# Two-layer hybrid encoder trunk on one core: the second half of the gated embedding moved behind the last expert, every expert's rows stored by the same transfer, and a reordered opening

## The chip, the cores and the metric

One core of a Trainium2 chip runs the whole program. The metric is device time in microseconds (us) of one execution. TensorE is written PE (PEld is its weight load), VectorE DVE, ScalarE ACT, GpSimd POOL and SyncE SP. SP issues most loads; POOL issues the indirect transfers and those that add into memory.

## The reference, cut to what is computed

512 tokens of width 1024 pass a layer norm and then two layers of this form:

```python
u = h @ w_in[i]                       # 1024 x 2560, three head groups
mix = concat([hyena, attention, pool]) @ w_out[i]
h = layer_norm(DN_ALPHA * h + mix, ln1_g[i], ln1_b[i])
y_moe = hier_moe(h, ...)              # 16 experts, every token goes to 2 of them
y_ple = sigmoid(h @ ple_wg[i] + ple_bg[i]) * (p[i] @ ple_wp[i])   # the gated embedding
h = layer_norm(DN_ALPHA * h + y_moe + y_ple, ln2_g[i], ln2_b[i])
```

An expert computes `silu(t @ w1) * (t @ w3) @ w2` with `w1`, `w3` of 1024x256 and `w2` of 256x1024, weighted by the token's gate.

## The kernel before, in words

Tokens are four tiles of 128 rows (`t` = 0 to 3). Matrix products keep nearly full float32 accuracy: `split` (L222) cuts a tensor into a rounded part `hi` (a cast on ACT) and a rest `lo` (a subtraction on DVE), and `mm3` (L215) issues three matmuls, hi x hi, hi x lo and lo x hi.

**Units.** All large weights are consumed through one list, made by `plan` (L1451). A unit is a weight slice of up to 512 KB, its loads and the matmuls that use it. `pump` (L233) issues the loads of the next units on SP and the splits of the next few; how far ahead is set by `ahead_raw` and `ahead_split`. In the expert stage this is 15 and 3 units (`P_MOE`), from expert 10 on 7 and 3 (`P_END`), from the last expert on 8 and 4 (`P_LAST`), where `cap` also stops the loads three units behind the end of the layer. `fill(n)` works off n units. Loaded slices, split parts, activations and norm gains share 34 slots of SBUF (`s4`). The compiler of the tile framework orders each engine's instructions; `behind()` and `issue_after` put instructions behind another one on the same engine's queue, without a wait between engines.

**Expert stage.** `layer` (L1518) gathers 128 rows of `h` per expert by an indirect transfer (`gather`, L1249), transposes them (`expert_x`), works four units of `w1` and `w3` (`add_expert_in`) and two of `w2` (`add_expert_out`). For experts 0 to 13 the result tile `ye` is added into the tensor `yd` in HBM by an indirect adding transfer on POOL (`scatter`, L1255). `yd` starts as a copy of the normed stream (`norm1`). The last two experts (`NL = 2`) stay on the core as two parts `yl`; `last_places` (L1414) makes one-hot matrices `hotT`, and `tail_sum` (L1420) brings their rows to the tokens with eight matmuls for each token tile (L1431), plus for the tiles in `ZPE` a float32 matmul with the identity (L1434).

**Gated embedding.** Each 512-column half of the gate has four units of 512 KB and 96 matmuls of 128x512. The first half (`add_ple(i, 0)`) comes ahead of the experts and is added into `yd` by two transfers of 512 KB on POOL (L1228). The second half is cut in two: two units after expert 3, kept in `plz`, and two after expert 12, then added into `yd` in the same way.

**End of a layer.** `load_stream` (L1407) reads `yd` back into `h` on POOL, after all that was added has landed. `finish` (L1441) then takes the tiles in turn: `tail_sum`, norm statistics (`moments`), the norm (`ln_tile`). In layer 0 these tiles feed the transposes and the projection of head 0 of layer 1 (`add_head` with `before`, L756), which works all four of its weight units for one tile before the next; in layer 1 they are stored to `out`.

**Opening.** `build` (L1640) issues on SP, in this order: tile 0 of `x` in two halves, gain and bias of the first norm as rows repeated over 128 partitions (`gain`, 512 KB each), the constants `cst` (409 KB, the identity for the transposes among them), the first head unit (384 KB), tiles 1 to 3 of `x`, and then the other units as they are pumped. Head 0 takes `start_norm` (L1492) for its norm; the statistics of tiles 1 to 3 are made on ACT directly behind tile 0. DVE clears five buffers at the start.

## Time and profile before

| | us |
|---|---|
| median of the runs | 1043.53 |
| lowest and highest of 3 runs | 1042.79 and 1048.24 |
| the profiled execution | 1045.37 |
| its span, first to last instruction | 1043.6 |

The page gives the busy time of each engine: PE 968.6 us, DVE 779.1, ACT 613.6, POOL 172.9. The span can be read as an opening up to 41.8 us (norm and head 0), the rest of layer 0's mixing part up to some 340 us, its expert stage up to 522.6 us, the passage into layer 1, the same parts again, the second expert stage up to 1016.1 us and a tail of 27.6 us. A window of the trace gives each engine's busy time and instruction count, the granted TensorE clock, and the mean busy share of the 16 DMA engines with the rate that they moved. Matmul records overlap, so the distance between two starts is the cost of one.

### The profile page before, as it was taken

How to read it: one execution, taken by the hardware profiler on the slowest of the kernel's cores; microseconds unless marked ns; L12 is line 12 of the kernel's file. 1: busy time of each engine (PE TensorE's matmuls, PEld its weight loads, DVE VectorE, ACT ScalarE, POOL GpSimd, SP SyncE). 2: the span in 40 equal slices, each digit the busy share in tenths (PEclk: the TensorE clock that was granted, in tenths of full speed). 3: DMA queues.
4: the chain of work that ended last, by engine and by line, in shares of the span. 5: the costliest groups of instructions: out<-in, count | busy, mean ns of one | idle time of the engine just before them, and what ended most of it. 6: DMA issues, size and time to landing. Idle time of an engine off the chain costs nothing. (4 is left out here: it accounts for less than half of the span.)

```text
span 1043.6 us, 14416 instructions
## 1 busy us (share of the span) xinstructions
PE 968.6 (93%) x4869; PEld 800.6 (77%) x4870; DVE 779.1 (75%) x1301; ACT 613.6 (59%) x1046; POOL 172.9 (17%) x170
## 2 busy tenths in 40 slices
PE   4999999999989999999979999999998999999995
PEld 3887889898767788777758889898776778877762
DVE  7576897777676778887865578847678587888785
ACT  5425464655653768886843346654655386888673
POOL 1101000000222222422121000000012222333121
PEclk9999999999999999999989999999999999999997
DMA  8816121222974999999974412122186399999974
GB/s 262 239 37 142 51 71 52 71 81 68 316 242 102 306 302 311 307 292 301 285 261 114 109 56 67 51 70 83 61 302 243 94 329 302 315 300 312 293 207 161
DMA packets 156010, 197.49 MB, mean 189 GB/s; under 512 B 20296, under 2 KB 123786, under 8 KB 155925
## 3 DMA queue, kind: packets, MB, share of 16 engines
q1 hardware_dynamic: 135253, 155.58, 45.5%
q0 software_dynamic: 20672, 40.87, 15.1%
q8 instruction: 42, 0.69, 0.3%
q14 instruction: 43, 0.35, 0.1%
HBM read 182.85 MB, written 29.36 MB: 203 GB/s over the span
## 5 line engine op out<-in xcount | busy, mean ns | idle before, releaser
L225 DVE TENSOR_TENSOR wlo<-raw,whi 128x1024 fp32r<-128x1024 f32 (+2 forms) x278 | 324.1, 1182 | 66.0 <-ACT whi L224 61.1
L224 ACT CAST whi<-raw 128x1024 fp32r<-128x1024 f32 (+2 forms) x278 | 277.9, 1024 | 33.1 <-DMA raw<-in_moe_w_dram 13.9
L218 PE MATMUL e<-whi,xT 128*128 128x512 f32 x256 | 106.6, 416 | 2.7 <-ACT xT L224 1.8
L219 PE MATMUL e<-wlo,xT 128*128 128x512 f32 x256 | 103.7, 405 | 0.1
L220 PE MATMUL e<-whi,xT 128*128 128x512 f32 x256 | 101.8, 398 | 0.0
L218 PE MATMUL pj<-whi,hT 128*128 128x384 f32 x256 | 90.0, 352 | 2.3 <-ACT hT L224 1.8
L219 PE MATMUL pj<-wlo,hT 128*128 128x384 f32 x256 | 88.2, 345 | 0.3 <-DVE wlo L225 0.3
L220 PE MATMUL pj<-whi,hT 128*128 128x384 f32 x256 | 87.3, 342 | 0.6 <-DVE hT L225 0.5
L1257 POOL DMA_INDIRECT yd<-ye,rt_tok x28 | 53.1, 1895 | 187.2 <-ACT ye L1323 66.7
L868 ACT ACTIVATE prob<-sc,mx 128x512 f32<-128x512 f32 x64 | 43.7, 688 | 39.1 <-DVE mx L867 36.6
L308 POOL TENSOR_TENSOR ors<-rs_y,mhalf 128x4 f32<-128x4 f32 x8 | 8.5, 1057 | 335.3 <-DVE rs_y L307 335.3
L1251 POOL DMA_INDIRECT xe<-hd,rt_tok x32 | 48.8, 1525 | 91.4 <-PE tr L376 48.1
L218 PEld LDWEIGHTS e<-whi,xT 128*128 128x128 f32 x256 | 48.9, 191 | 12.9 <-ACT xT L224 2.2
L219 PEld LDWEIGHTS e<-wlo,xT 128*128 128x128 f32 x256 | 48.8, 191 | 11.4 <-DVE wlo L225 2.4
L220 PEld LDWEIGHTS e<-whi,xT 128*128 128x128 f32 x256 | 48.8, 191 | 10.0
L219 PE MATMUL e<-wlo,actT 128*128 128x512 f32 x128 | 51.6, 403 | 3.1 <-DVE wlo L225 3.1
L218 PE MATMUL mo<-whi,YT 128*128 128x512 f32 x128 | 53.2, 415 | 0.0
L218 PEld LDWEIGHTS pj<-whi,hT 128*128 128x128 f32 x256 | 48.9, 191 | 4.8 <-ACT hT L224 2.5
L219 PE MATMUL pl<-wlo,hT 128*128 128x512 f32 x128 | 51.4, 401 | 1.1 <-DVE wlo L225 1.1
L218 PE MATMUL pl<-whi,hT 128*128 128x512 f32 x128 | 50.8, 402 | 0.6 <-ACT whi L224 0.5
L218 PE MATMUL e<-whi,actT 128*128 128x512 f32 x128 | 47.8, 398 | 3.8 <-ACT whi L224 2.9
L218 PE MATMUL pj<-hT,whi 128*128 128x512 f32 x128 | 51.2, 404 | 0.0
(340 smaller groups left out, 2313.1 us busy)
## 6 DMA issues: line engine op xcount, KB each, us to landing
raw<-in_moe_w_dram SPq DMA_DIRECT2D x256, 256.0 KB
raw<-in_moe_w_dram SPq DMA_DIRECT2D x64, 512.0 KB
raw<-in_w_in_dram SPq DMA_DIRECT2D x96, 128.0 KB
raw<-in_w_in_dram SPq DMA_DIRECT2D x16, 512.0 KB
raw<-in_ple_wg_dram SPq DMA_DIRECT2D x16, 512.0 KB
raw<-in_w_out_dram SPq DMA_DIRECT2D x14, 512.0 KB
tabi<-c_tabi_dram POOLq DMA_DIRECT2D x8, 516.0 KB, 4.6
tabf<-c_tabf_dram POOLq DMA_DIRECT2D x8, 512.0 KB
```

The lines of the kernel that those rows point to most:

```text
L218: mm(ps, a[0], b[0], start=start, stop=False)
L219: mm(ps, a[0], b[1], start=False, stop=False)
L220: mm(ps, a[1], b[0], start=False, stop=stop)
L224: self.nc.scalar.copy(hi, src)
L225: self.nc.vector.tensor_sub(lo, src, hi.bitcast(F32))
L308: nc.gpsimd.tensor_tensor(out, y, self.mhalf[:, :n], op=OP.pow)
L868: nc.scalar.activation(p[:, c], o, AF.Exp, bias=mx[:, c:c + 1], accum_out=sm[:, c:c + 1])
L1251: self.nc.gpsimd.indirect_dma_start(out=x, out_offset=None, in_=self.hd[:, :], in_offset=bass.IndirectOffsetOnAxis(ap=tok, axis=0), bounds ...
L1257: self.nc.gpsimd.indirect_dma_start(out=self.yd[:, :], out_offset=bass.IndirectOffsetOnAxis(ap=row, axis=0), in_=y, in_offset=None, bounds ...
```

## The change

- **Gated embedding.** The second half is no longer cut in two. Its four units follow the last expert's; the matmuls start when all four are split, one token tile after the other (24 matmuls each). The gated product stays on the core: it overwrites `pwp[1]`, and `tail_sum` adds it to `h`. The two adding transfers of this half are gone, and the first half's `plz` and the experts' `ye` share two buffers (`out4`).
- **Experts.** All sixteen store by `scatter`. `NL`, `last_places`, `own`, `yl`, `hotT` and `ZPE` with all their matmuls are gone. `load_stream` is issued behind the last expert's store and ahead of the second half's four units. `tail_sum` makes one column half's sum on ACT and adds the gated product to the other on DVE; tile 0's is queued on ACT and DVE behind the gating of token tile 2.
- **Opening.** SP issues tile 0 of `x`, two single rows of gain and bias (4 KB each), the 128 identity columns of `cst`, all four units of head 0 (two loads each in place of three, the same rows), tiles 1 to 3 of `x`, and then the rest of `cst`. PE repeats the two rows over the partitions by four float32 matmuls with a row of ones, ACT copies them out. The statistics of tiles 1 to 3 and the split of the gate weights are queued behind casts of weights; four memsets go from DVE to POOL; two small constants are made later.

```diff
 def ple_tile(self, t, c, z, o):
+    g = z if c else o
+    nc.vector.tensor_add(g, z, self.bg[:, c * 512:(c + 1) * 512])
+    act = nc.scalar.activation(g, g, AF.Tanh, scale=0.5)
+    dve = nc.vector.scalar_tensor_tensor(o, g, 1.0, self.pwp[c][t // 2][:, t % 2], op0=OP.add, op1=OP.mult)
+    self.gated[c, t] = act.ins, dve.ins
...
 def add_ple(self, i, c):
+    def second(q):
+        def f(wp):
+            st["w"].append(wp)
+            if q < 3:
+                yield 0.01
+                return
+            for t in range(NT):
+                ps = self.ps("pl")
+                for n, x in enumerate(st["w"]):
+                    mms(ps, t, n, x)
+                self.ple_tile(t, c, ps, self.pwp[c][t // 2][:, t % 2])
+                yield 5.12
+        return f
...
 def tail_sum(self, i, t):
-    with self.behind():
-        for c in range(2):
-            for e in range(NE - NL, NE):
-                for x in range(2):
-                    nc.tensor.matmul(ps, self.hotT[e][:, t], self.yl[e][x][:, cs], ...)
-            if t in self.ZPE[i]:
-                nc.tensor.matmul(ps, self.ident, h[:, cs], start=False, stop=True)
-                nc.scalar.activation(h[:, cs], ps, AF.Copy, accum_out=sums[:, c:c + 1])
-                continue
-            nc.vector.scalar_tensor_tensor(h[:, cs], h[:, cs], 1.0, ps, ...)
+    with contextlib.ExitStack() as order:
+        if t == 0:
+            for ins in self.gated[1, 2]:
+                order.enter_context(self.tc.issue_after(ins))
+        else:
+            order.enter_context(self.behind())
+        nc.scalar.activation(self.s2([128, 512], "lnsq", BF16), h[:, :512], AF.Copy, accum_out=sums[:, 0:1])
+        nc.vector.scalar_tensor_tensor(h[:, 512:], h[:, 512:], 1.0, self.pwp[1][t // 2][:, t % 2], op0=OP.mult,
+                                       op1=OP.add, accum_out=sums[:, 1:2])
...
 def plan(self, i):
     for e in range(NE):
         self.add_expert_in(i, e)
         if e > 0:
             self.add_expert_out(i, e - 1)
-        if e in self.PLE_AT:
-            self.add_ple(i, 1, self.PLE_AT.index(e))
     self.add_expert_out(i, NE - 1)
+    self.add_ple(i, 1)
...
 def layer(self, i):
         self.fill(2)
+        self.load_stream()
+        self.fill(4)
...
 def build(self):
             if t == 0:
-                self.gb = self.gain(A["ln0_g"], A["ln0_b"])
-                nc.sync.dma_start(self.cst, self.C["cst"])
-                self.pump(0, -1)
+                for src in (A["ln0_g"], A["ln0_b"]):
+                    r = self.s4([128, 1024], "grow")
+                    nc.sync.dma_start(r[0:1], bass.AP(tensor=src.tensor, offset=src.offset, ap=[[0, 1], [1, 1024]]))
+                    rows.append(r)
+                nc.sync.dma_start(self.cst[:, :128], self.C["cst"][:, :128])
+                self.pump(3, -1)
+        nc.sync.dma_start(self.cst[:, 128:], self.C["cst"][:, 128:])
         self.setup()
+        for r in rows:
+            g = self.s4([128, 1024], "gain")
+            for c in range(2):
+                cs = slice(c * 512, (c + 1) * 512)
+                ps = self.ps("gb")
+                nc.tensor.matmul(ps, self.ones[0:1], r[0:1, cs], start=True, stop=True)
+                nc.scalar.copy(g[:, cs], ps)
```

## Rows read from the trace of the kernel before

**Rows 1.** The page's part 1: busy us, share of the span and instructions by engine.

```profile
PE 968.6 (93%) x4869; PEld 800.6 (77%) x4870; DVE 779.1 (75%) x1301; ACT 613.6 (59%) x1046; POOL 172.9 (17%) x170
```

**Rows 2.** Windows of 20 us: start:end length, busy by engine (instructions), clock, DMA share, GB/s.

```profile
0.00:20.00 20.00, 4.60 (x14) 3.18 (x15) 13.03 (x22) 8.46 (x18) 3.24 (x11) 1.00 0.86 271
...
60.00:80.00 20.00, 20.00 (x92) 16.08 (x92) 15.14 (x25) 4.15 (x6) 0.00 (x0) 1.00 0.16 46
...
380.00:400.00 20.00, 20.00 (x96) 16.42 (x95) 14.85 (x19) 11.47 (x16) 4.18 (x3) 1.00 0.86 273
...
460.00:480.00 20.00, 18.07 (x84) 13.68 (x82) 16.14 (x18) 14.46 (x20) 6.22 (x4) 1.00 0.95 297
...
520.00:540.00 20.00, 13.68 (x42) 8.40 (x42) 12.01 (x21) 8.49 (x16) 3.00 (x6) 0.83 1.02 333
```

**Rows 3.** Waits of PE up to 45 us: what ended them, us in all, times, longest.

```profile
PE tr L376 <- DMA cst<-c_cst_dram: 11.4, 1, 11.4
```

**Rows 4.** Timeline of head 0: start, us, engine, line, instruction, idle before it and its releaser.

```profile
13.91 0.69 PE L218 MATMUL pj<-whi,hT 128*128 128x384 f32 x1 [0.55 <-ACT whi L224]
...
23.11 0.84 ACT L224 CAST whi<-raw 128x768 fp32r<-128x768 f32 x1
23.39 0.52 PE L219 MATMUL pj<-wlo,hT 128*128 128x384 f32 x1
23.71 0.52 PE L220 MATMUL pj<-whi,hT 128*128 128x384 f32 x1
...
25.68 0.34 PE L218 MATMUL pj<-whi,hT 128*128 128x384 f32 x1
25.86 0.34 PE L219 MATMUL pj<-wlo,hT 128*128 128x384 f32 x1
...
42.02 0.37 ACT L797 COPY uqk<-pj 128x256 f32<-128x256 f32 x1 [1.72 <-PE pj L220]
```

**Rows 5.** Timeline of ACT in layer 0's expert stage: experts 1 and 2, a late weight.

```profile
354.62 0.38 ACT L1274 ACTIVATE act<-e 128x256 f32<-128x256 f32 x1 [0.18 <-PE e L220]
...
364.05 0.39 ACT L1274 ACTIVATE act<-e 128x256 f32<-128x256 f32 x1
...
474.60 1.05 ACT L224 CAST whi<-raw 128x1024 fp32r<-128x1024 f32 x1 [2.22 <-DMA raw<-in_moe_w_dram]
```

**Rows 6.** DMA queues in 464 to 478 us: packets, MB, share of the 16 engines' time.

```profile
q1 hardware_dynamic: 1658, 3.33, 67.8%
q0 software_dynamic: 437, 0.80, 27.0%
```

**Rows 7.** The same in 492 to 506 us, in which the adding transfers of `plz` run.

```profile
q1 hardware_dynamic: 2142, 2.83, 61.9%
q0 software_dynamic: 544, 1.05, 44.0%
```

**Rows 8.** Timeline of PE: last matmuls of expert 15 in both layers, head 0 of layer 1.

```profile
522.15 0.40 PE L220 MATMUL e<-whi,actT 128*128 128x512 f32 x1
...
541.24 0.34 PE L218 MATMUL pj<-whi,hT 128*128 128x384 f32 x1
...
1015.42 0.39 PE L219 MATMUL e<-wlo,actT 128*128 128x512 f32 x1
1015.65 0.40 PE L220 MATMUL e<-whi,actT 128*128 128x512 f32 x1
```

**Rows 9.** Groups by line: count | busy us, mean ns of one | idle before.

```profile
L1434 PE MATMUL el<-h,cst 128*128 128x512 f32 x16 | 10.2, 725 | 6.2 <-DMA h<-yd 6.2
L1207 ACT ACTIVATE plz<-plz 128x512 f32<-128x512 f32 x16 | 9.9, 632 | 36.6 <-DVE plz L1206 36.6
```

**Rows 10.** Timeline of the tail: first sum of tile 0 and last part of tile 3's norm.

```profile
1020.66 0.69 DVE L1437 SCALAR_TENSOR_TENSOR h<-h,el 128x512 f32<-128x512 f32 x1 [2.86 <-DMA h<-yd]
...
1038.27 1.41 DVE L350 SCALAR_TENSOR_TENSOR h<-ln,lnrs,gain 128x512 f32<-128x512 f32 x2 [0.82 <-POOL lnrs L308]
```

**Rows 11.** The instructions of line 1257 (an expert's store): time from issue to landing.

```profile
DMA to landing us min/median/max: 8.5/8.9/9.7
```

More of the change, by code (lines that the diff above doesn't have):

```diff
@@ L25 @@
 NE = 16
-NL = 2
 ALPHA = (2 * DEPTH) ** 0.25
@@ L205, in s2, with out4 @@
                                      padded_shape=[128, HALF * 4 // mybir.dt.size(dt)]), shape)
+    def out4(self, shape, name):
+        n = int(np.prod(shape[1:]))
+        return _view(self.slots.tile([128, n], F32, name=name, tag="out4", bufs=2), shape)
     def ps(self, name):
@@ L222, in split @@
     def split(self, hi, lo, src):
-        self.nc.scalar.copy(hi, src)
+        self.cast = self.nc.scalar.copy(hi, src).ins
         self.nc.vector.tensor_sub(lo, src, hi.bitcast(F32))
@@ L399, in setup @@
         nc.vector.memset(self.ones, 1.0)
-        self.tri_b = self.cp.tile([128, 128], BF16, name="tri_b")
-        nc.vector.tensor_copy(self.tri_b, cst[:, C_TRI:C_TRI + 128])
-        self.ones_b = self.cp.tile([128, 128], BF16, name="ones_b")
-        nc.vector.memset(self.ones_b, 1.0)
         self.qL = self.cp.tile([128, 2, 512], F32R, name="qL")
-        nc.vector.memset(flat(self.qL).bitcast(F32), 0.0)
+        nc.gpsimd.memset(flat(self.qL).bitcast(F32), 0.0)
     def setup_late(self):
@@ L421, in setup_late @@
         self.pw = self.cp.tile([128, DEPTH * 2, 128], F32, name="pw")
-        nc.vector.memset(self.pw, 0.0)
+        nc.gpsimd.memset(self.pw, 0.0)
         for half in range(2):
@@ L431, in setup_late @@
             x = self.xp.tile([128, 1024], F32, name="xe", tag="xe")
-            nc.vector.memset(x, 0.0)
+            nc.gpsimd.memset(x, 0.0)
     def lam(self):
         nc, A = self.nc, self.A
+        self.tri_b = self.cp.tile([128, 128], BF16, name="tri_b")
+        with self.behind():
+            nc.vector.tensor_copy(self.tri_b, self.cst[:, C_TRI:C_TRI + 128])
+        self.ones_b = self.cp.tile([128, 128], BF16, name="ones_b")
+        nc.vector.memset(self.ones_b, 1.0)
         lq = self.s2([128, 2, 2, 2, 64], "lq")
@@ L1018, in gate_weights @@
         gw = self.sm.tile([128, 8, 2, 20], F32R, name="gwhl", bufs=1)
-        self.split(gw[:, :, 0], gw[:, :, 1], raw)
+        with self.behind(), self.tc.issue_after(self.cast):
+            self.split(gw[:, :, 0], gw[:, :, 1], raw)
         self.gate = gw, gb
@@ L1212, in add_ple @@
+    def add_ple(self, i, c):
         nc = self.nc
         cs = slice(c * 512, (c + 1) * 512)
[L1214 to L1229 removed]
@@ L1241, in f @@
                     yield 1.28
             return f
-        for q in qs:
+        def second(q):
[11 more added lines that the diff above has]
+            return f
@@ L1245, in add_ple @@
+        for q in range(4):
             src = self.A["ple_wg"][i][q * 256:(q + 1) * 256, cs].rearrange("(k p) n -> p k n", p=128)
-            self.add([(lambda r: r, src)], [2, 512], emit(q))
+            self.add([(lambda r: r, src)], [2, 512], (first, second)[c](q))
     def gather(self, tok):
@@ L1308, in f @@
                              [x[:, c * 512:(c + 1) * 512] for x in wp], k == 0, k == 1)
[L1309 to L1321 removed]
+                if k == 1:
+                    y = self.out4([128, 1024], "ye")
                     for c in range(2):
@@ L1497, in start_norm @@
                 self.ln(self.h[0], self.h[0], self.gb, self.ln_stats(self.h[0]), True)
-                self.stats = [None] + [self.ln_stats(self.h[u]) for u in range(1, NT)]
+                with self.tc.issue_after(self.cast):
+                    self.stats = [None] + [self.ln_stats(self.h[u]) for u in range(1, NT)]
             else:
@@ L1647, in build @@
         self.h = []
+        self.cst = self.cp.tile([128, C_N], F32, name="cst")
+        rows = []
         for t in range(NT):
```

91 lines of the change are left out of this document (25 added, 66 removed).

## The prediction

> **What bounds the kernel now.** I read the page's busy times first. PE is busy 968.6 of 1043.6 us, DVE 779.1, ACT 613.6 [rows 1]. So some 75 us of PE's time are idle; the rest of the span can only shrink if PE's work shrinks, and only where PE is what a stage waits for. Next I read windows of 20 us, to see where the idle time lies [rows 2]: 15.4 us stand in the first window, 6.3 in 520 to 540 (the passage into layer 1), a like stretch at the end, and a few us in the second half of each expert stage, where the DMA share is 0.95 or more. These are the places that the change touches. Then I asked what ended the waits in each.
>
> In the opening PE waits 11.4 us for `cst` [rows 3]. The first projection starts at 13.91, the cast of the fourth head weight starts only at 23.11, and the last token tile of head 0 is copied out at 42.02 [rows 4].
>
> In the expert stage two streams run side by side: PE with 9.4 us for an expert (364.05 - 354.62 [rows 5]), and the 16 DMA engines. From about 460 us on ACT waits for weights to land, here 2.2 us at 474.6 [rows 5], with some nine more up to the end of the stage; PE has 1.9 us of idle time in that window while the DMA share is 0.95 [rows 2]. The lead of loaded weights is used up there: from then on the stage moves at the pace of the loads, not of PE. This is the point on which the prediction turns.
>
> **The opening.** Before, about 5.1 MB stand ahead of the fourth head weight on SP's queue (x 2.1, gain and bias 1.05, `cst` 0.42, head 1.57). After, it is 2.2 MB (tile 0 of x 0.52, identity 0.07, head 1.57, two rows). At the 271 GB/s of the first window [rows 2] that is 19 us against 8, so the weights come at 10 to 11 us in place of 23. What replaces the repeated loads: four float32 matmuls of one row by 512 columns. The nearest row is the identity matmul L1434: two records for each of 8 matmuls, 10.2 us in all, 1.28 us each [rows 9]. Records overlap (0.39 long at a distance of 0.23 [rows 8]), so 0.75 to 1.28 us of PE, and up to twice that at half the clock. I take 1.7, as PE is slow at the start, so 6.8 us for four, with bounds of 3 and 10. The rows come right behind tile 0's 0.5 MB, by an estimate at 4 us, so the last copy is out at 11.5 (8 to 15); then come the norm's last half, the transposes, and the first projection at about 12.4 against 13.91. The real gain is that tile 0's 24 matmuls then run without a wait.
>
> What they cost depends on the clock. Before, two starts of 128x384 lie 0.32 us apart at 23.39 and 0.18 us apart from 25.68 on [rows 4], so the engine was at 1.2 GHz first and at 2.4 after it had been busy without a long gap; the granted column reads 1.00 in both, so here the distance tells the level. Tile 0 takes 7.7 us at the one, 4.2 at the other. Then three tiles at 24 x 0.175 + 1.0 for the transposes, 5.2 us, or 5.6 with gaps, since ACT and DVE also have their norms to make. Head 0 ends at 33.5 to 37 in place of 42: a gain of 5 to 8.5, and I take 7. It lives on, as PE has no idle time from 60 to 80 us [rows 2]; if the loads behind it (forward tables, Hyena weights) can't follow, down to 4 of it are left. The Trainium skill, "TensorE: Matmul & The Clock Gate" (Part 1), says that the engine's clock is throttled by default and that activity releases it; the new matmuls would thus wake the engine ahead of tile 0, and the gain would be 8.5. The rows of this trace show the same rise, but no case with such matmuls in front.
>
> The other edits of the opening cost nothing that lasts. The four memsets wait on POOL in front of nothing but the norm's two small POOL steps and, much later, the gathers; a memset of the same size is under 1 us on DVE, and even 3 us on POOL end before tile 0's statistics do. The queue edges (`issue_after`) make no engine wait for another; the statistics of tiles 1 to 3 start at 11 us on ACT, and tile 1's norm is ready at 17, when PE is still on tile 0. On SP tiles 1 to 3 of x come behind the head weights and land at about 11 to 15 us, ahead of their use.
>
> **The expert stage: how much earlier is the last expert (call it s)?** PE loses the 96 matmuls of the two parts. Their distance is 20 us / 92 = 0.217 with few loads [rows 2], 0.23 among loads [rows 8], so 20.8 to 22 us go. If PE set the pace s would be 20.8. But the loads set it, and they lose less. The four units are 2.1 MB; at 67.8% of 14 us for 3.33 MB [rows 6], 2.85 us of all engines for 1 MB, they cost 6.0 us. The two adding transfers are 1.05 MB and took 44.0% of 14 us [rows 7], 6.2 us (at the plain price 3.0, the lower bound). Expert 14's store is added ahead of the end: 64 rows, 0.26 MB, at 4.7 to 5.9 us for 1 MB 1.2 to 1.5 us. In 380 to 400 PE was busy with the first part, the slots stayed full and the share was 0.86 [rows 2]; up to 2.8 us of load time come back there. Sum: 6.0 + 6.2 - 1.3 = 10.9, with the last item up to 13.7, and with the adding transfers at the plain price 7.5. I take s = 11.5, for both layers. PE will stand idle some 9 us more in the second half of each stage than before. The Trainium skill, "DMA: Bandwidth & Descriptors" (Anatomy of one DMA), gives a transfer 2 us and its bytes at 436 GB/s; by it the two adds occupy the engines for 2.4 us, and s would be about 7. The row of this trace says 6.2, and I go by it.
>
> **What lies behind the last expert.** Before, layer 1 ends 1043.6 - 1016.05 = 27.55 us behind expert 15's last matmul [rows 8], mostly the store's landing, the reload of `yd` and four tiles of norm. After, the second half stands first. Its weights follow the last expert's in SP's queue and land 6 us behind them; the fourth unit is needed 4 us into tile 0, so they cost 1 us at most. Token tiles 0 to 2 are 72 x 0.23 = 16.6 us; the gating of tile 2 is two DVE steps of 0.69 (as the sum in rows 10, of the same shape) around 0.63 on ACT [rows 9], with handing over 2.2. Meanwhile the last store lands (8.9 us [rows 11]) and `h` is read back, some 18 us behind the last expert: hidden by those 19, with 1 us to spare. On POOL these reads stand ahead of the norm's small steps, which need them anyway. Then four tiles of norm. Before they took 1020.66 to 1039.68, 19.0 us [rows 10]; the sums no longer wait for PE, but DVE has 0.69 for the sum and twice 1.41 for the norm in each [rows 10], 3.5, and tile 3's gating of 1.4 between; with the first tile's wait for its statistics that is 17 us at the least. I take 18. Then 3.9 us for the last store to `out`, as before. In all 0.2 + 16.6 + 2.2 + 18 + 3.9 = 40.9 us behind the last expert: 13.3 more than before. So layer 1's end moves by 13.3 - s, which is +1.8.
>
> In the passage into layer 1 the first projection came 541.24 - 522.55 = 18.7 us behind the last expert [rows 8]. After: 0.2 + 16.6 + 2.2, then 5.5 us of sum, square, POOL steps, half a norm, transposes and cast: 24.5, or 5.8 more. Between the later tiles eight matmuls of L1431 go, 1.8 us at 0.23, of which 1.3 are taken as they also hid a wait. Change 4.5 - s, which is -7.0. The clock, granted at 0.83 in 520 to 540 [rows 2] where PE was waiting, costs nothing here, as PE has work up to the norm.
>
> **Sum.** -7 (opening) - 7 (passage) + 1.8 (tail) = -12.2 us. The profiled execution took 1045.37 with a span of 1043.6, and the median is 1043.53; the sum is made on the span and I take it off the median: 1031.3, so 1031. In general the change is 17.8 - 2s minus the opening's gain.
>
> **The rivals.**
> 1. PE sets the expert stage after all: the loads catch up, as the share is not at its peak (1.02 in 520 to 540 at 333 GB/s [rows 2]). s = 20.8, and the time is 1043.5 - 7 + 17.8 - 41.6 = 1013. Against it: the waits for weights of rows 5 exist already with the slower PE pace.
> 2. The adding transfers were cheap (s = 7.5) and the opening gives 4: 1043.5 - 4 + 17.8 - 15 = 1042. The skill's price for a transfer points here; the fall of the plain queue beside them in rows 7 speaks against it.
> 3. Slower: the last expert is not earlier at all. The loads keep the same end time, since what was removed is made up by stores and loads bunched at the end, and PE's 22 us then simply stand behind it. At s = 0 it is 1043.5 - 7 + 17.8 = 1054; it decides from s below 2.8 on. For it: the stage ends on loads now [rows 5]. Against it: SP's queue serves its loads in order, so 2.1 MB less ahead of the last expert bring it forward.
> 4. The opening does not shorten head 0 (ACT and DVE queues bind instead of the loads): 1043.5 - 5.2 = 1038.
>
> **How the numbers follow.** Forecast 0.50, its own range 1023 to 1037; rival 1 0.17, rival 2 0.16, rival 3 0.09, rival 4 0.08. About 0.5%, 5.2 us, is what a measurement can tell from no change. Faster: nearly all of the forecast (0.47), rival 1 and half of rival 4, 0.68. Within: rival 2, the rest of 4 and 0.02 to 0.03 of the forecast, 0.22. Slower: rival 3 with a little beside it, 0.10. The range reaches from 1014 (s near 20) to 1043 (just beyond rival 2).
>
> **What would show it.** Right: head 0 copied out at 34 to 37 us; fourth head cast before 12; waits of ACT for expert weights longer and earlier than at 460; expert 15's last matmul 10 to 13 us earlier relative to the stage's start; the second half as one block of 21 to 22 us of dense PE work; 40 us from the last expert to the end. Wrong: if PE has no added idle time in the expert stage (rival 1), if the last expert keeps its distance from the stage's start (rival 3), or if the norm of tile 0 waits for `h` and not for the gating.

## The result, and where the time went

The changed kernel is slower: 1054.6 us median (1051.9 to 1060.4 in 4 runs) beside 1043.9 of the kernel before on the same chip, ratio 1.0118, 95% interval 1.0093 to 1.0144. The forecast was 1031, its range ended at 1043, and 0.10 was given to a loss of this size. The profiled execution took 1052.93 us with a span of 1051.2.

The page of the changed kernel, its busy times; PE works 6.8 us less than in [rows 1] and the span is 7.6 longer:

```profile
PE 961.8 (92%) x4797; PEld 790.7 (75%) x4798; DVE 764.1 (73%) x1275; ACT 615.6 (59%) x1050; POOL 177.2 (17%) x174
```

Windows of 20 us of the changed kernel, for PE alone: start:end, length, PE's busy time and instructions, granted clock, DMA share, GB/s. They answer to [rows 2].

```profile
0.00:20.00 20.00, 13.51 (x30) 1.00 0.89 248
20.00:40.00 20.00, 14.00 (x69) 0.83 0.63 187
...
460.00:480.00 20.00, 15.53 (x65) 1.00 0.90 281
```

The second window of the kernel before (all engines: PE, PEld, DVE, ACT, POOL, clock, DMA share, GB/s):

```profile
20.00:40.00 20.00, 19.44 (x104) 18.76 (x105) 14.78 (x20) 12.57 (x26) 5.50 (x8) 1.00 0.87 238
```

The first window looks better than before, 13.5 us of PE work in place of 4.6, but 7.2 of these are the new matmuls that repeat the gain rows. The second is where the opening loses: 14.0 us with a clock of 0.83, where before it was 19.4 of 20. In the second half of the expert stage PE has more idle time, as forecast: 4.5 us from 460 to 480 in place of 1.9.

To see where the 7.6 us come from I cut the span at the starts of five PE records. Timeline of PE in the changed kernel: start, us, engine, line, instruction, idle before it and its releaser.

```profile
342.96 0.50 PE L220 MATMUL e<-whi,xT 128*128 128x512 f32 x1 [0.82 <-ACT xT L226]
...
518.44 0.40 PE L222 MATMUL e<-whi,actT 128*128 128x512 f32 x1
...
544.89 0.44 PE L220 MATMUL pj<-whi,hT 128*128 128x384 f32 x1
...
834.92 0.50 PE L220 MATMUL e<-whi,xT 128*128 128x512 f32 x1 [0.30 <-ACT xT L226]
...
1010.68 0.39 PE L222 MATMUL e<-whi,actT 128*128 128x512 f32 x1
```

In the kernel before the same five records start at 335.58, 522.15, 541.24, 831.38 and 1015.65. The second, third and last are those of [rows 8]; these are the first and the fourth:

```profile
335.58 0.50 PE L218 MATMUL e<-whi,xT 128*128 128x512 f32 x1 [0.93 <-ACT xT L224]
...
831.38 0.50 PE L218 MATMUL e<-whi,xT 128*128 128x512 f32 x1 [0.83 <-ACT xT L224]
```

The differences are the stages:

| stage | before | after | change | forecast |
|---|---|---|---|---|
| opening and mixing of layer 0 | 335.6 | 343.0 | +7.4 | -7 |
| expert stage 0, first to last expert matmul | 186.6 | 175.5 | -11.1 | -11.5 |
| passage into layer 1 | 19.1 | 26.4 | +7.4 | +5.8 |
| mixing of layer 1 | 290.1 | 290.0 | -0.1 | -1.3 |
| expert stage 1 | 184.3 | 175.8 | -8.5 | -11.5 |
| tail | 27.9 | 40.5 | +12.6 | +13.3 |
| sum | 1043.6 | 1051.2 | +7.6 | -12.2 |

The opening missed by 14.4 of the 19.8 us, the second expert stage by 3.0, the passage by 1.6. The other lines are within 1.2.

**The opening.** Rows of the changed kernel, from the timelines of PE, ACT and DVE in turn:

```profile
4.47 7.16 PE L1659 MATMUL gb<-grow,ones 1*128 1x512 f32 x8 [4.47 <-DMA grow<-in_ln_g_dram]
...
14.69 1.11 PE L378 MATMUL tr<-cst,h 128*128 128x128 f32 x4 [2.02 <-DVE h L338]
15.46 0.67 PE L220 MATMUL pj<-whi,hT 128*128 128x384 f32 x1
15.92 0.52 PE L221 MATMUL pj<-wlo,hT 128*128 128x384 f32 x1
16.24 0.60 PE L222 MATMUL pj<-whi,hT 128*128 128x384 f32 x1
...
28.03 1.97 PE L378 MATMUL tr<-cst,h 128*128 128x128 f32 x8 [5.87 <-DVE h L338]
```

```profile
11.66 0.59 ACT L1660 COPY gain<-gb 128x512 f32<-128x512 f32 x1 [1.12 <-PE gb L1659]
...
16.32 0.83 ACT L226 CAST whi<-raw 128x768 fp32r<-128x768 f32 x1
19.49 1.05 ACT L226 CAST whi<-raw 128x1024 fp32r<-128x1024 f32 x1 [2.33 <-DMA raw<-in_w_in_dram]
20.44 0.63 ACT L361 ACTIVATE lnsq<-h 128x512 bf16<-128x512 f32 x1
...
48.02 0.37 ACT L800 COPY uqk<-pj 128x256 f32<-128x256 f32 x1 [1.66 <-PE pj L222]
```

```profile
13.01 0.96 DVE L227 TENSOR_TENSOR wlo<-raw,whi 128x768 fp32r<-128x768 f32 x1 [1.63 <-ACT whi L226]
13.89 0.75 DVE L338 SCALAR_TENSOR_TENSOR h<-h,lnrs,gain 128x512 f32<-128x512 f32 x1
...
26.69 1.28 DVE L338 SCALAR_TENSOR_TENSOR h<-h,lnrs,gain 128x1024 f32<-128x1024 f32 x1 [0.57 <-POOL lnrs L310]
```

Read from the bottom: tile 1's norm is ready only at 28.0 (26.69 + 1.28), so PE, done with tile 0 at 22.2, waits 5.87 us. Its statistics start on ACT at 20.44. In front of them stands a cast of 128x1024, which is no head weight (those are 128x768) but the first Hyena weight: it waited 2.33 us for its load. `issue_after(self.cast)` named that cast, because a unit of the Hyena had been split ahead before head 0 was emitted. And at 13.89 the second half of tile 0's norm stands on DVE behind the difference of the first head weight, 1.6 us after the last gain copy ended (12.25). That is half of what the first projection is late, 15.46 in place of 12.4; the rest is a copy 0.75 us later than forecast and a way from the norm to the projection of 1.6 us, where 0.9 had been allowed. The fourth head cast stands at 16.32, where the prediction's sign was before 12. Head 0 is out at 48.0 where it was 42.0 [rows 4].

**The passage.** POOL's rows in the changed kernel, and ACT's first sum of tile 0:

```profile
506.89 1.63 POOL L1267 DMA_INDIRECT yd<-ye,rt_tok  x1 [8.51 <-ACT ye L1322]
516.41 2.60 POOL L1267 DMA_INDIRECT yd<-ye,rt_tok  x1 [7.89 <-ACT whi L226]
526.34 1.55 POOL L1267 DMA_INDIRECT yd<-ye,rt_tok  x1 [7.33 <-ACT pl L1206]
533.23 0.60 POOL L1411 DMA_DIRECT2D h<-yd  x1 [5.34 <-DVE pwp L1207]
```

```profile
539.36 0.63 ACT L1425 ACTIVATE lnsq<-h 128x512 bf16<-128x512 f32 x1 [2.46 <-DMA h<-yd]
```

Expert 15's rows were ready on ACT at 521.0 (its last copy starts at 520.32), yet their store went out at 526.34, 9.9 us behind expert 14's store, and `h` was asked for 6.9 us behind that. The releasers that the rows name are not what held them, as e14_apart shows below. What these issues have in common is the tensor `yd`; the experiments come back to it. So in the passage tile 0's norm waits for `h`, 2.46 us, not for the gating: the sign that the prediction named as wrong. In layer 1's tail `h` is there before tile 2 is gated.

### The profile page after: what moved, and what is told of

Its sections match the earlier page's. It is cut to its first block, busy times and chain, and to the rows that moved or that the text cites. A ratio compares the mean times of both kernels' runs of the same rounds, so it can differ in the third digit from the quotient of the medians.

```text
span 1051.2 us, 14172 instructions
## 1 busy us (share of the span) xinstructions
PE 961.8 (92%) x4797; PEld 790.7 (75%) x4798; DVE 764.1 (73%) x1275; ACT 615.6 (59%) x1050; POOL 177.2 (17%) x174
## 5 line engine op out<-in xcount | busy, mean ns | idle before, releaser
L221 PE MATMUL e<-wlo,xT 128*128 128x512 f32 x256 | 106.3, 415 | 3.4 <-DVE wlo L227 3.2
L1267 POOL DMA_INDIRECT yd<-ye,rt_tok x32 | 59.4, 1857 | 228.5 <-ACT ye L1322 139.6
L220 PE MATMUL pj<-whi,hT 128*128 128x384 f32 x256 | 91.4, 357 | 1.4 <-ACT hT L226 1.4
L222 PE MATMUL pj<-whi,hT 128*128 128x384 f32 x256 | 88.9, 348 | 0.6 <-DVE hT L227 0.5
L1322 ACT ACTIVATE ye<-e,rt_gate 128x512 f32<-128x512 f32 x64 | 43.6, 690 | 27.4 <-PE e L222 27.1
```

The costliest lines, as they stand in the source:

```text
L220: mm(ps, a[0], b[0], start=start, stop=False)
L221: mm(ps, a[0], b[1], start=False, stop=False)
L222: mm(ps, a[1], b[0], start=False, stop=stop)
L1267: self.nc.gpsimd.indirect_dma_start(out=self.yd[:, :], out_offset=bass.IndirectOffsetOnAxis(ap=row, axis=0), in_=y, in_offset=None, bounds ...
L1322: nc.scalar.activation(y[:, c * 512:(c + 1) * 512], st["ps"][c], AF.Copy, scale=self.gates[:, e:e + 1])
```

## The experiments

Theory A: the opening loses by itself, through what is queued in front of the statistics; the embedding's part is near zero. Theory B: the gain matmuls delay the opening. Theories L, S, C and Y come with their runs. All ratios are to the kernel before on the same chip, with 95% intervals, which reach some 2 us to either side.

| kernel | median us | ratio | interval |
|---|---|---|---|
| changed kernel | 1054.6 | 1.0118 | 1.0093 to 1.0144 |
| open_only | 1050.1 | 1.0064 | 1.0047 to 1.0082 |
| gate_only | 1047.6 | 1.0047 | 1.0028 to 1.0066 |
| late_hy | 1051.5 | 1.0078 | 1.0062 to 1.0094 |
| gain_dma | 1055.9 | 1.0116 | 1.0096 to 1.0136 |
| open2 | 1050.5 | 1.0059 | 1.0033 to 1.0084 |
| open3 | 1047.8 | 1.0052 | 1.0032 to 1.0073 |
| x_first | 1043.0 | 1.0000 | 0.9984 to 1.0015 |
| one_load | 1049.6 | 1.0062 | 1.0039 to 1.0086 |
| late0 | 1044.5 | 1.0004 | 0.9984 to 1.0024 |
| no_adds | 1029.8 | 0.9873 | 0.9850 to 0.9896 |
| e12_apart | 1038.5 | 0.9953 | 0.9934 to 0.9972 |
| e14_apart | 1046.7 | 1.0043 | 1.0022 to 1.0063 |
| keep_z | 1032.2 | 0.9887 | 0.9869 to 0.9905 |
| keep_zz | 1039.9 | 0.9950 | 0.9928 to 0.9972 |

The stages of the profiled executions, cut as above (us):

| kernel | to first expert | stage 0 | passage | mixing 1 | stage 1 | tail |
|---|---|---|---|---|---|---|
| before | 335.6 | 186.6 | 19.1 | 290.1 | 184.3 | 27.9 |
| open_only | 339.8 | 187.2 | 20.2 | 291.8 | 182.7 | 28.8 |
| open2 | 340.5 | 187.2 | 18.8 | 289.7 | 184.0 | 28.6 |
| open3 | 340.9 | 185.8 | 18.7 | 290.7 | 183.6 | 28.6 |
| x_first | 332.5 | 187.0 | 17.8 | 290.1 | 184.3 | 28.6 |
| changed | 343.0 | 175.5 | 26.4 | 290.0 | 175.8 | 40.5 |
| gate_only | 334.3 | 174.9 | 26.4 | 290.9 | 178.2 | 40.0 |
| late_hy | 340.0 | 176.4 | 26.4 | 295.7 | 175.7 | 40.3 |
| gain_dma | 343.0 | 176.2 | 26.2 | 291.4 | 176.9 | 40.4 |
| one_load | 335.0 | 178.9 | 24.5 | 291.4 | 175.4 | 40.8 |
| e14_apart | 336.3 | 175.1 | 24.3 | 293.7 | 177.4 | 40.0 |
| late0 | 334.9 | 175.2 | 28.0 | 292.9 | 188.4 | 24.0 |
| no_adds | 333.7 | 183.4 | 14.5 | 289.9 | 180.5 | 25.4 |
| e12_apart | 335.7 | 188.7 | 18.8 | 291.0 | 184.4 | 23.7 |
| keep_z | 332.0 | 185.2 | 14.5 | 288.7 | 180.9 | 24.9 |
| keep_zz | 335.8 | 188.2 | 13.2 | 290.4 | 184.3 | 27.0 |

Kernels of the same arrangement repeat a stage to 1 to 2.5 us (late_hy's mixing of layer 1, 295.7, apart), which says how far one profile can be trusted. Each profile is of one execution: those of late_hy (1056.3 us) and e12_apart (1044.0) are the slowest of theirs, that of keep_z (1028.0) is the fastest of its six.

**The two parts apart.** open_only is the kernel before with the opening's lines, gate_only the kernel before with the rest.

```diff
 open_only, in build()
-                self.gb = self.gain(A["ln0_g"], A["ln0_b"])
-                self.cst = self.cp.tile([128, C_N], F32, name="cst")
-                nc.sync.dma_start(self.cst, self.C["cst"])
-                self.pump(0, -1)
+                for src in (A["ln0_g"], A["ln0_b"]):
+                    ...
+                nc.sync.dma_start(self.cst[:, :128], self.C["cst"][:, :128])
+                self.pump(3, -1)
```

> The opening's edits alone, with the gated embedding, the experts' rows and the tail as before. Theory A: the opening itself lost the time (in the changed kernel the first expert matmul stood at 342.96 us in place of 335.58, 7.4 later), so this kernel is 6 to 8 us slower than before, 1050 to 1052, with head 0 copied out near 48 us. Rival: the first 340 us of the changed kernel are late because of something the gated embedding's edits did to buffers or queues; then this kernel shows the gain I forecast, 1036 to 1040, and head 0 is out at 34 to 37.

> The gated embedding's second half behind the last expert and all experts' rows by store, with the opening as before. Theory A: what is left of the changed kernel's difference without its opening: passage 7.6 - 11.3, layer 1's start -0.1, its expert stage and tail -8.5 + 12.6, together 0.3, so 1044 and no measurable difference. My own forecast's terms for this part gave -5.2, 1038. Rival: this part is the loser by itself, 1050 or more.

open_only is 6.7 us slower and gate_only 4.9, together 11.6, which is the changed kernel's 12.3: the parts add up. The opening loses about what theory A said. The embedding's part loses too, more than the ledger of one profile promised.

**What in the opening.** late_hy and gain_dma each change one thing in the changed kernel.

```diff
 late_hy
-        self.ahead_raw, self.ahead_split, self.cap = 4, 2, 1 << 30
+        self.ahead_raw, self.ahead_split, self.cap = 4, 0, 1 << 30
 gain_dma, in build()
-                for src in (A["ln0_g"], A["ln0_b"]):
-                    ...
+                self.gb = self.gain(A["ln0_g"], A["ln0_b"])
```

> The changed kernel with one number changed: no Hyena weight is cast ahead while head 0 is prepared, so that the statistics of tiles 1 to 3 stand on ACT right behind the fourth head cast. Theory A (ACT, held by the first Hyena cast that waits for its load until 19.5 us, kept the statistics back): statistics of tile 1 start at about 17.2 in place of 20.4, PE's wait of 5.9 us behind tile 0 shrinks to 1 or 2, head 0 is out at 42 to 44, and the time is 4 to 6 us below the changed kernel, 1048 to 1050. Theory B (the four matmuls that repeat the gain rows, with ACT's copies, are what delays everything): head 0 stays at 47 to 48 and the time at 1053 to 1055.

> The changed kernel with gain and bias loaded repeated (1.05 MB at the same place in the queue) in place of rows and matmuls; the edge of the statistics stays. Theory A: the head weights and x land about 4 us later, the statistics still stand behind the Hyena cast, so head 0 is out at 47 to 51 and the time is that of the changed kernel or up to 3 us more. Theory B: without the matmuls the first projection starts at 12 to 13 in place of 15.5, head 0 is out 3 us earlier and the time is 1050 to 1051.

In late_hy the statistics of tile 1 start right behind the fourth head cast, and its norm comes at 22.1 in place of 26.7 (timelines of ACT and DVE):

```profile
17.16 0.63 ACT L361 ACTIVATE lnsq<-h 128x512 bf16<-128x512 f32 x1
```

```profile
22.11 1.28 DVE L338 SCALAR_TENSOR_TENSOR h<-h,lnrs,gain 128x1024 f32<-128x1024 f32 x1 [0.56 <-POOL lnrs L310]
```

It is some 4 us faster than the changed kernel, as theory A wanted; head 0 is out at 46.2, though, where 42 to 44 was expected. gain_dma starts its first projection at 12.9, but its statistics stand behind the same Hyena cast and start at 22.8; it gains nothing. So theory B falls as the cause of the loss, and the cast that waited for its load is one cause. A small price of the gain matmuls is not excluded, since gain_dma's longer loads also bring that Hyena cast 2.4 us later. It is not the whole: late_hy without the embedding's 4.9 would still be 3 us slower than before. open2 therefore took the Hyena cast, the gain matmuls and DVE's copy of the triangle out of the way.

```diff
 open2, against open_only
+                self.gb = self.gain(A["ln0_g"], A["ln0_b"])
-        self.ahead_raw, self.ahead_split, self.cap = 4, 2, 1 << 30
+        self.ahead_raw, self.ahead_split, self.cap = 4, 0, 1 << 30
-        with self.behind():
+        with self.tc.issue_after(self.head_last):
             nc.vector.tensor_copy(self.tri_b, self.cst[:, C_TRI:C_TRI + 128])
```

> The opening alone again (embedding and tail as before), with the three things that held ACT, PE and DVE taken away: gain and bias are loaded repeated, no Hyena weight is cast ahead while head 0 is prepared, and the bf16 copy of the triangle is made behind the norms. The head weights still stand in front. Theory A (the reordered loads are worth what I forecast, and only what was queued in front of the statistics spoiled it): first projection at 12.9, statistics of tile 1 from about 15.7, tile 0 complete near 20, and the time 4 to 6 us below before, 1037 to 1039. Rival (loads put in front only push those behind them back, so the Hyena weights and the tables are late instead): within 2 us of before, 1041 to 1045, although head 0 is earlier.

Neither came: it lost 6 us all the same. open2's rows, from the timelines of ACT and PE and its windows (all engines: PE, PEld, DVE, ACT, POOL, clock, DMA share, GB/s):

```profile
16.23 0.63 ACT L359 ACTIVATE lnsq<-h 128x512 bf16<-128x512 f32 x1 [0.38 <-DMA h<-in_x_dram]
```

```profile
19.41 0.34 PE L220 MATMUL pj<-whi,hT 128*128 128x384 f32 x1
22.47 1.09 PE L376 MATMUL tr<-cst,h 128*128 128x128 f32 x8 [2.72 <-DVE h L336]
...
27.06 0.52 PE L218 MATMUL pj<-whi,hT 128*128 128x384 f32 x1
27.38 0.52 PE L219 MATMUL pj<-wlo,hT 128*128 128x384 f32 x1
```

```profile
20.00:40.00 20.00, 15.40 (x76) 14.17 (x77) 12.15 (x17) 10.99 (x25) 6.23 (x9) 0.83 0.91 253
```

What the forecast wanted of tile 0 is there: the first projection at 13.07, its 24 matmuls done at 19.41 with no wait over 0.31 us. But x of tile 1 lands only at 16.2, behind the head weights, and its norm is ready at 22.4. PE waits 2.72 us, and its next projections, with two shorter waits between them, run at a distance of 0.32 us up to 30.6, where tile 0's last ones had stood 0.175 apart. The granted clock of that window is 0.83. Before, PE had its gap early, and from 25.5 on no gap of note and a distance of 0.175 [rows 4]. Theory C put the blame on the order of the loads and on this second price of a gap:

```diff
 x_first, against open2 (open3 has only the second edit)
-                self.pump(3, -1)
+                self.pump(0, -1)
...
+        self.pump(3, -1)
         nc.sync.dma_start(self.cst[:, 128:], self.C["cst"][:, 128:])
...
-                with self.tc.issue_after(self.cast):
-                    self.stats = [None] + ...
+                self.stats = [None] + ...
```

> open2 with tiles 1 to 3 of x loaded behind the first head weight and ahead of the other three, and their statistics not tied to a cast (before's order of loads, with the identity in front of the rest of the table). Theory C (tile 1's norm, not the head weights, decides when PE can go on behind tile 0; every gap there costs a second time, since PE's next matmuls run at a distance of 0.32 us in place of 0.175): the loss of open2 is gone, PE has no gap of over 1 us behind tile 0's last matmul, and the time is 1041 to 1045. Rival (the loss is in the other edits of the opening: memsets on POOL, head weights in two transfers, the split table): 1048 to 1051 as in open2.

> open2 without the edge that ties the statistics of tiles 1 to 3 to a cast; x still behind all head weights. It stands between open2 and x_first, which differ in two things. Theory C1 (the order of the loads decides: x behind the head weights comes too late): 1047 to 1050, with a gap of 2 to 3 us behind tile 0 as in open2. Theory C2 (the edge decides, since with it ACT makes all four head casts and DVE all four differences before the first statistics): 1042 to 1045 as in x_first.

x_first: ACT's first statistics, PE's waits in the timeline, the second window.

```profile
12.46 0.63 ACT L359 ACTIVATE lnsq<-h 128x512 bf16<-128x512 f32 x1 [10.41 <-DMA h<-in_x_dram]
```

```profile
16.18 0.69 PE L218 MATMUL pj<-whi,hT 128*128 128x384 f32 x1 [4.32 <-ACT whi L224]
17.65 0.69 PE L219 MATMUL pj<-wlo,hT 128*128 128x384 f32 x1 [0.78 <-DVE wlo L225]
```

```profile
20.00:40.00 20.00, 19.53 (x112) 18.28 (x111) 16.13 (x29) 13.01 (x25) 6.43 (x8) 1.00 0.80 212
```

The loss is gone with the order of the loads (1.0000), and not with the edge alone (open3, 1.0052): theory C1 stands, and the memsets, the two loads for each head weight and the split table, which x_first keeps, are not the loss. x_first's first projection is the latest of all, 16.18, and head 0 is out at 41.3, as early as before: past 18 us PE has no wait over 0.3 us, and the clock is 1.00. The granted column alone is no sure sign here: open3's second window reads 1.00 too, though its projections stand 0.32 apart up to 29.8 and head 0 is out at 46.3. x_first says also what the forecast's aim was worth: nothing is gained in it either, with the identity and the last three head weights ahead of the rest of the table.

**What in the embedding.** Theory L: the second half's weights, loaded behind the last expert's, end layer 1. one_load drops three of these four loads and casts.

```diff
 one_load, against gate_only
-            self.add([(lambda r: r, src)], [2, 512], (first, second)[c](q))
+            self.add([] if c and q else [(lambda r: r, src)], [2, 512], (first, second)[c](q))
...
-                st["w"].append(wp)
+                st["w"].append(wp or st["w"][0])
```

> gate_only, in which the second half loads and casts only its first weight and uses it for all four parts: 1.57 MB of loads and three casts are left out in each layer (the values are then others). Theory L (the weights of the second half decide the end of layer 1: they are still on their way when expert 15 is done, and ACT's cast of the first of them stands in front of the cast of expert 15's activations): in layer 1 the time from expert 15's activation to the last matmul falls from 12.1 us to the 6.6 of layer 0, tile 2 is gated 3 to 5 us earlier, and the time is 4 to 6 us below gate_only, 1042 to 1044. Rival (the weights cost 1 us at most, as I forecast): within 1 us of gate_only, 1046.5 to 1048.

It gained nothing; stage and tail of layer 1 are 216.2 us together where gate_only has 218.2 and the changed kernel 216.3. So the three loads and casts that it drops decide nothing. But it keeps the first of the four, and in layer 1 that one's cast stands on ACT in front of the cast of expert 15's activations. ACT and PE of the changed kernel, and PE of one_load:

```profile
1004.41 1.04 ACT L226 CAST whi<-raw 128x1024 fp32r<-128x1024 f32 x1 [0.51 <-DMA raw<-in_ple_wg_dram]
1005.36 0.37 ACT L226 CAST actT<-e 128x256 fp32r<-128x256 f32 x1
```

```profile
1005.78 0.50 PE L220 MATMUL e<-whi,actT 128*128 128x512 f32 x1 [3.45 <-ACT actT L226]
```

```profile
1001.31 0.50 PE L220 MATMUL e<-whi,actT 128*128 128x512 f32 x1 [3.76 <-ACT actT L226]
```

PE's wait for these activations is 3.25 to 3.82 us in layer 1 of the four kernels of the new arrangement and 0.93 to 0.94 in their layer 0, where that cast comes behind the activations. So the part of theory L that blames the order of the casts was not tested; no run takes this cast away. late0 has the new arrangement in layer 0 only (layer 1 takes the methods of the kernel before, by `if i not in self.LATE`):

> The second half behind the last expert in layer 0 only; layer 1, its tail and the opening as before. By the ledger of gate_only's profile the edit takes about 4 us from layer 0 (first projection of layer 1 at 535.6 in place of 541.2, of which 1.3 stood already ahead of the first expert) and gives some 5 to 8 back in layer 1. Theory A: so layer 0 alone is a gain, 1039 to 1040. Rival (both layers lose alike, 2 us each): 1045 to 1046.

It stands level with before (1.0004, so theory A's 1039 to 1040 is excluded). By stages, against the means of the five old kernels, layer 0 wins 2.5 us up to layer 1's start, not 4, and the mixing of layer 1 took 2.4 more in that execution. Layer 1 is where gate_only's loss lies: its stage and tail are 216.0 to 218.2 us in the four kernels of the new arrangement, 211.5 to 212.9 in the five of the old.

no_adds asks what the adding transfers cost, the largest and least certain term of my s.

```diff
 no_adds, against before
-                if t % 2:
+                if t % 2 and part is None:
                     nc.gpsimd.dma_start(self.yd[...], z, accum_op=OP.add)
```

> The kernel before without the two adding transfers of the second half (1.05 MB in each layer; that half of the embedding is left out of the result). My forecast took 6.2 us for them in each layer: 12 us less in all, 1031. By the plain price of the queue beside them, 3.0 us each layer, it is 1037. If loads don't set the stage there at all, 1043 and no change.

By the ratio it is 13.3 us in all (10.9 to 15.7; the medians lie 14.5 apart), about the 12.4 of the forecast. But the stages put part of it elsewhere: against the mean of the five old kernels (186.8, 18.9, 183.8, 28.5) the expert stages are only 3.4 and 3.3 us shorter, and 4.4 and 3.1 are in passage and tail. The two stages of no_adds, PE alone: start:end, length, busy (instructions), clock, DMA share, GB/s:

```profile
333.73:517.11 183.38, 177.79 (x823) 0.99 0.96 303
821.55:1002.04 180.49, 177.02 (x824) 0.99 0.92 294
```

PE is busy in all but 5.6 and 3.5 us of them (7.1 and 6.9 before), so these stages could hardly get shorter with its matmuls still in them. The 3.4 and 3.3 us are what PE's own work let through, and not all the time that the loads may have lost. Theory Y: the writes to `yd` and its read-back form a chain. POOL in the kernel before, and PE's longest wait there:

```profile
493.11 1.33 POOL L1228 DMA_DIRECT2D yd<-plz  x1 [8.32 <-DVE plz L1208]
495.52 1.19 POOL L1228 DMA_DIRECT2D yd<-plz  x1 [1.09 <-DVE plz L1208]
506.89 2.38 POOL L1257 DMA_INDIRECT yd<-ye,rt_tok  x1 [10.18 <-DMA yd<-plz]
517.77 1.58 POOL L1257 DMA_INDIRECT yd<-ye,rt_tok  x1 [8.50 <-DMA raw<-in_w_in_dram]
525.18 1.83 POOL L1412 DMA_DIRECT2D h<-yd  x3 [5.83 <-DMA raw<-in_w_in_dram]
```

```profile
PE el L1434 <- DMA h<-yd: 3.6, 1, 3.6
```

Expert 12's rows were ready at 501.8 and went out at 506.89, when the adds had landed; expert 13's followed 10.9 us later and `h` 7.4 behind those. Not every pair waits: the two adds, which go to different rows of `yd`, went out 2.4 us apart. e12_apart and e14_apart take one link out of the chain, before and in gate_only.

```diff
 e12_apart (e14_apart: 14, against gate_only)
-                    self.scatter(y, self.rows[:, e:e + 1])
+                    self.scatter(y, self.rows[:, e:e + 1], self.yz if e == 12 else self.yd)
```

> The kernel before with expert 12's rows stored to another tensor in DRAM (they are left out of the result). The adding transfers of the second half stay. Theory Y (what writes to one tensor waits for the landing of the write before: the two adds, then expert 12's rows, expert 13's, then the read-back of h, 8 to 10 us each; this chain ends the passage and the tail): h is asked for at about 518 in place of 525, PE's wait for it goes, passage and tail are 3 to 4 us shorter each, 1036 to 1038. Rival (the price of the adding transfers is all time of the DMA engines): 1042 to 1044, passage and tail as before.

> gate_only with expert 14's rows stored to another tensor in DRAM (they are left out of the result). Theory Y: expert 15's store goes out when its rows are ready, 5 us earlier, h is there before tile 2 is gated, and the passage is 1.7 to 2 us shorter in layer 0; in layer 1 h came 3 us ahead of the gating already, so nothing changes there: 1045 to 1046.5. Rival (the store was held by something else): passage 26.4 as before, 1047 to 1048.

e14_apart, POOL:

```profile
508.35 1.55 POOL L1265 DMA_INDIRECT yz<-ye,rt_tok  x1 [6.87 <-ACT actT L226]
513.91 1.82 POOL L1265 DMA_INDIRECT yd<-ye,rt_tok  x1 [4.00 <-DMA raw<-in_w_in_dram]
```

The two stores go out 5.6 us apart, where 9.3 lay between them in gate_only and 9.9 in the changed kernel, and expert 15's goes out 0.3 us after its rows are ready (513.63). The passage is 24.3 us in place of 26.4, layer 1's tail 40.0 as before, both as theory Y had it; in the time the 2 us are too small to tell (1.0043 beside 1.0047). e12_apart is 4.9 us faster than before (2.9 to 6.9), a little short of the 6 to 8 expected. Its tail is 23.7 in place of 28.5; its passage is not shorter, although PE no longer waits for `h` there. Why, is not settled, and its profile is of its slowest execution. So the chain is real, and with one link less layer 1's tail is 4.8 us shorter. How much of no_adds' 13.3 us is this chain and how much the transfers' own time, no run separates.

**A version that beats both.** If the adds cost some 13 us and moving the matmuls behind the last expert gives that away, the sum should be made on the chip and the matmuls left where they were.

```diff
 keep_z, against before (keep_zz: for both halves)
+        w = self.pwp[c][t // 2][:, t % 2]
-        nc.vector.scalar_tensor_tensor(o, o, 1.0, self.pwp[c][t // 2][:, t % 2], op0=OP.add, op1=OP.mult)
+        nc.vector.scalar_tensor_tensor(w if c else o, o, 1.0, w, op0=OP.add, op1=OP.mult)
...
-                if t % 2:
+                if t % 2 and not c:
...
 in tail_sum
+                if c:
+                    nc.tensor.matmul(ps, self.ident, self.pwp[c][t // 2][:, t % 2], start=True, stop=False)
```

> The kernel before, in which the gated second half isn't added in DRAM but stays on the chip (it overwrites the product it is gated with, two slots held to the end of the layer) and is summed in the tail by an identity matmul in each token tile. Its matmuls stay at experts 3 and 12. Theory S (the adding transfers are what the expert stage pays for; no_adds showed 14.5 us for both layers, and moving the matmuls behind the last expert gave that gain away again): 1030 to 1035, the 1029.8 of no_adds plus up to 2.5 us in each layer for four identity matmuls. Rival (two slots fewer from expert 12 on shorten the lead of the loads, and the gain is lost): 1038 to 1044.

> keep_z with both halves kept on the chip: no adding transfer at all, four slots held through the expert stage, two identity matmuls in each tile of the tail. Theory S: the first half's transfers (1.05 MB a layer) run at the start of the expert stage, where the loads have a lead, so they are worth less than the 7 us of the second: 1026 to 1032. Rival (four slots fewer for the loads all through the stage): slower than keep_z, 1034 to 1045.

keep_z takes 1032.2 us, by the ratios 11.8 below before and some 24 below the changed kernel, as theory S had it. POOL of keep_z:

```profile
515.89 1.82 POOL L1413 DMA_DIRECT2D h<-yd  x3 [6.62 <-PE e L220]
```

`h` is asked for 9.3 us earlier than before, and the passage is 14.5 us long. keep_zz gives more than half of it back, and theory S's 1026 to 1032 missed: with both halves kept, its expert stages are 3.0 and 3.4 us longer than keep_z's in the two profiles. Two more slots held all through the stage may be the reason; no run separates it from others.

## Why the prediction was wrong, step by step

**The opening: the sign.** The opening was to gain 7 us and lost 7.4. The steps up to the gain rows were right: four float32 matmuls took 7.2 us (6.8 forecast), the last copy was out at 12.2 (11.5). Three steps failed.

1. "The queue edges (`issue_after`) make no engine wait for another; the statistics of tiles 1 to 3 start at 11 us on ACT, and tile 1's norm is ready at 17, when PE is still on tile 0." They started at 20.44 and the norm was ready at 28.0. An edge puts work behind one instruction of its own engine and behind everything that this instruction waits for. I didn't ask which cast `self.cast` was when the statistics were emitted. late_hy put some 4 us on it.
2. "On SP tiles 1 to 3 of x come behind the head weights and land at about 11 to 15 us, ahead of their use." In open2, with no Hyena cast in front of the statistics, tile 1 lands at 16.2 and its norm is ready 6.2 us after that, when PE had been done with tile 0 for 2.7 us. x_first against open3 shows that this order alone is worth 5 us.
3. "It lives on, as PE has no idle time from 60 to 80 us": true, but it holds for a loss too. And a gap has a second price that I had in hand: [rows 4] show the distance of 0.32, and I used it for tile 0 alone. In the changed kernel the projections behind the wait of 5.87 us stand 0.32 apart again, up to 33.8.

By the Trainium skill, "TensorE: Matmul & The Clock Gate" (Part 1), which has activity release the clock, the new matmuls in front of tile 0 would have made the gain 8.5. The trace doesn't show it: behind 7.2 us of them, and a wait of 2.02 us, tile 0's first matmuls stand at 15.92 and 16.24, 0.32 apart. Nor is it the wait alone: the four transposes at 11.56, right behind the new matmuls, start 0.21 apart, where later ones (41.34) start 0.11 apart.

The range was at fault as well: "down to 4 of it are left" had no end on the other side, though the part adds a wait. Rival 4 priced the failure at no gain.

**s, how much earlier the last expert is.** 11.5 was forecast for both layers. By the means of the five old and the four new kernels it is 11.0 in layer 0 and 7.1 in layer 1. The mechanism held: PE lost 17 to 18 us of work in each stage, but its idle time there grew from 7.1 to 14.3 us and from 6.9 to 15.5, so the loads set the pace and rival 1 (20.8) is excluded. What failed is the step "I take s = 11.5, for both layers": layer 1 is 4.4 short. About 2.6 of these stand in PE's wait for expert 15's activations, 3.5 us there and 0.94 in layer 0, for which the sum had no term; that s would be so much larger without it is argued, not shown, and the rest is open.

The size of the adding transfers, 6.2, is not settled. The share of 44% in [rows 7] counts time in which the engines held those transfers (with the loads' 61.9% it makes over 100%), not time that the loads lost; no_adds' 3.3 us are held down by PE's own work. With 3.3 the sum would be 8.0, with 6.2 it is 10.9, where layer 0 came out. (With the plain price of 3.0 it is 7.7; I wrote 7.5.) By the Trainium skill, "DMA: Bandwidth & Descriptors" (Anatomy of one DMA), I had worked out 2.4 as an estimate, and s about 7. Layer 1 came out there, but by the wait for the activations at least in part, and no run here shows the price of these transfers by itself.

**Behind the last expert.** 40.9 us were forecast behind the end of the last expert's matmuls, 40.1 came (40.5 in the table, which counts from a start): 18.1 to the end of tile 2's gating (19.0), 22.1 from there (21.9). The gating of tile 2, DVE in the changed kernel:

```profile
1028.46 0.69 DVE L1207 SCALAR_TENSOR_TENSOR pwp<-pl,pwp 128x512 f32<-128x512 f32 x1 [0.71 <-ACT pl L1206]
```

In the passage the step "hidden by those 19, with 1 us to spare" failed by some 2 us: the landing of 8.9 us [rows 11] was counted once, but the last store also waits for the landing of the one before. e14_apart returned 2.1 us of passage.

**The sum.** With the means in place of the terms, the embedding's part is -11.0 + 7.4 + 1.5 - 7.1 + 11.8 = +2.6 where -5.2 was forecast; gate_only measured 4.9 (2.9 to 6.9). The 2 us between are within what single profiles vary by; most of the 1.5 of mixing is late_hy's one execution. The time came out at rival 3's 1054, but not by rival 3: there the last expert wasn't to be earlier at all, and it was, by 7 to 11 us. That the two agree is chance: more than half of the loss is the opening's, which rival 3 left at a gain of 7.

## What to carry to other kernels

Before you move a load or an edge forward, write down for each engine's queue what then stands in front of the next thing that PE needs, and give the step a negative end: here a cast that waited for its load held statistics that needed nothing of it. The gap of 2.72 us on PE in open2 cost twice, since the matmuls behind it ran at half the pace; x_first, whose PE starts 3.1 us later and then hardly waits, was 6 us faster. Where several transfers write one tensor in DRAM and it is read back, count the landings in a row; keeping one summand on the chip (keep_z) was worth 11.8 us, and the reordering nothing. And before you read a price off a run that leaves work out, look how much idle time the busiest engine has in that stage: no_adds could show little more than PE's 7 us.

## What the runs showed of the hardware

- In these programs the experts' indirect stores into one tensor went out one landing apart: 9.5 and 9.9 us between the changed kernel's last three of layer 0 (their landings took 6.1 to 10.8 us, the median 9.0), 5.6 between two that went to different tensors. Shown for POOL's queue, on which all of them stand.
- Adding transfers of 1.05 MB took 44.0% of the DMA engines for 14 us [rows 7]. Without them the expert stages were 3.4 and 3.3 us shorter, with PE busy in all but 5.6 and 3.5 us of what was left, and passage and tail 4.4 and 3.1.
- Behind a wait of 2.72 us (open2) PE's projections stood 0.32 us apart in place of 0.175 for several us, and behind 5.87 us (changed kernel) likewise, each with 0.83 granted in that window; in x_first, with no wait over 0.3 us past 18 us, it reads 1.00. A wait of 1.19 us did not decide it: in open2 (at 39.10) the projections behind it stand 0.32 apart, in late_hy (at 40.11) soon 0.175.
- Eight matmul records with one contraction row, 7.2 us of them, left PE at the slow pace: the transposes right behind them start 0.21 us apart, later ones 0.11.
